# A matmul with a decayed running sum: the opening sixteen steps rearranged in banks, pieces and order

## The chip, the cores and the metric

The kernel runs on one core of a Trainium2 chip. Its time is the device time of one execution in microseconds (us), the median over several executions; lower is better. The profile is one execution recorded by the hardware profiler, and all instants below count from the start of its span.

## The reference

```
x: (16, 2048, 1024)  w: (1024, 1024)  decay: (1024,)      float32
xw = x @ w
out[:, 0] = xw[:, 0]
for t in range(1, 2048):
    out[:, t] = decay * out[:, t - 1] + xw[:, t]
```

So there is one large matrix product and, along each batch's time axis, a first-order recurrence in every one of the 1024 output columns.

## The kernel before

**Tiling.** The 16 x 2048 rows of x are cut into 64 chunks of 512 rows, and two neighbouring chunks make a group. The 1024 output columns are cut into eight heads of 128 (n = 0 to 7; head n belongs to half h = n // 4 of the columns). The contraction is cut into eight blocks k = 0 to 7, where k = 2m + e: m is one of four column blocks of x, and e says which of two interleaved columns it is. One step is one head of one group: sixteen matmuls of 128 x 512 (eight k, two chunks) into a PSUM tile of two banks. There are 248 such steps, and the last group is worked chunk by chunk in 16 half-size steps. Products have the output columns on the partitions and time along the free axis, so the recurrence is a scan along the free axis.

**PSUM.** Three two-bank tiles turn in a ring named `ps`; `spare` is one bank, and `dec2`, the squared decay, takes the eighth bank. In the first group, heads 0 to 2 use the three `ps` tiles, and head 3 has `spare` for its first chunk and the next tile of the `ps` ring for its second.

**Engines.** POOL issues the loads of x with a cast to bf16 (L105, four DMAs for a chunk, one for each quadrant of the partitions) and most of the loads of w (L245). VectorE (DVE) turns a chunk by 32 x 32 blocks (L115, 32-bit elements, so pairs of bf16 stay together), and a copy parts the pairs into the layout that TensorE reads (L123): on ScalarE (ACT) in the steady state, and split between ACT and DVE in the first two chunks. w lands in staging tiles and is "settled" into its place by sixteen copies (L253), numbered 8h + 4e + m; copy number i must be there before the heads of half h can use block k = 2m + e.

**After the matmuls** a tile goes one of two ways. Unpaired: DVE scans all of it straight out of PSUM (L194). Paired: ACT copies it to `xs` (L168) and scales its even columns by the decay into `h` (L158), POOL adds (L174), DVE scans the odd columns alone with the squared decay (L180), ACT scales that result (L158), and POOL adds the even columns (L208). A PSUM tile is free after the scan L194, or after the pair L168 and L158. Heads 3 and 7 are unpaired, heads 0 and 1 of the first group too. Then DVE turns the result back (L215), and SP stores four heads at a time with four DMAs (L228).

**Order.** Every instruction is pinned to program order, and each engine runs its own instructions strictly in that order. The order of all work but the matmuls is written by hand for the first 17 steps, in the dictionary `agenda` (L320); step 8 has an empty entry. Entry -99 comes ahead of all steps; entry s comes behind the matmuls of step s. Later steps follow a fixed rule (`usual`). The letters: M loads half a chunk of x, U a part of w, L the next quadrant of a later chunk. W and w settle a piece of w on DVE and on ACT. E turns half a chunk; F (DVE) and G (ACT) part it. T turns a whole chunk, X and Y part its two halves on ACT. P is the ACT and POOL work ahead of a scan, S the scan, C what completes a tile, B the turn back, D makes the decay columns and their squares.

**The opening.** 34 matmuls on zeros (L262) keep TensorE busy until the first data. Then, for chunk 0, heads 0 to 3: the even k of its first half, the even k of its second half, and the odd k over its full width. Then heads 0 to 2 of chunk 1 by halves, and head 3 of chunk 1 (step 3). Step 4 is the first that uses the second half of w.

Of the kernel before, what the change touches and what calls it, by code (L numbers as in the profile page):

```python
# [25 lines left out]
def kernel(  # L26
# [63 lines left out]
    dec2 = psp.tile([128, 512], FP32, name="dec2")  # L90
# [19 lines left out]
    def turn(c, j0=0, j1=NJ):  # L110
        if c not in xw_of:
            xw_of[c] = ring(sb, "xw", 2, [128, M, NJ, P, 2], BF16)
        src = xb_of[c][:, j0:j1].rearrange("p j c -> p (j c)").bitcast(FP32)
        dst = xw_of[c].rearrange("p m j i e -> p (m j i e)").bitcast(FP32)
        pin(nc.vector.transpose(  # L115
            out=dst.rearrange("p (m j i) -> p j m i", m=M, i=P)[:, j0:j1],
            in_=src.rearrange("p (j m c) -> p j m c", m=M, c=P)))
# [18 lines left out]
    class Tile:  # L136
# [3 lines left out]
        def __init__(self, g, n, ps, ot, there):  # L140
            self.b, self.t0 = chunks[g[0]]
            self.T = TL * len(g)
            self.n, self.ps, self.ot, self.there = n, ps, ot, there
            self.final = g == [nch - 1]
            self.paired = n % R != R - 1
            if len(tiles) in flips or len(tiles) - len(slots) in flips:
                self.paired = not self.paired
            self.so = ring(sb, "so", 4, [128, 2 * TL + 2])
            self.prev = None if self.t0 == 0 else last[n]
            if self.t0 + self.T < S:  # L150
                last[n] = const.tile([128, 1], FP32, name=f"keep{n}", bufs=2)
                self.keep = last[n]
            else:
                self.keep = None
# [22 lines left out]
        def scan(self):  # L177
            T, n, so = self.T, self.n, self.so
            if self.paired:
                pin(nc.vector.tensor_tensor_scan(  # L180
                    out=so[:, 3:T + 2:2],
                    data0=dec2[:, n:n + 1].to_broadcast([128, T // 2]),
                    data1=self.xs[:, 1:T:2],
                    initial=0.0 if self.prev is None else self.prev,
                    op0=ALU.mult,
                    op1=ALU.add,
                ))
            else:
                parts = self.ps if isinstance(self.ps, tuple) else (self.ps,)
                size = T // len(parts)  # L190
                before = 0.0 if self.prev is None else self.prev
                for i, ps in enumerate(parts):
                    t = 2 + i * size
                    pin(nc.vector.tensor_tensor_scan(  # L194
                        out=so[:, t:t + size],
                        data0=dec[:, n:n + 1].to_broadcast([128, size]),
                        data1=ps,
                        initial=before,
                        op0=ALU.mult,
                        op1=ALU.add,  # L200
                    ))
                    before = so[:, t + size - 1:t + size]
# [10 lines left out]
        def back(self):  # L213
            T, n = self.T, self.n
            pin(nc.vector.transpose(  # L215
                out=self.ot[:, :, n % R * P:(n % R + 1) * P],
                in_=self.so[:, 2:T + 2].rearrange("p (i t) -> p i t", t=P)))
            self.there.add(n)
            size = 2 if self.final and n >= R else R
            n0 = n // size * size  # L220
            if self.there.issuperset(range(n0, n0 + size)):
                self.store(n0, n0 + size)

        def store(self, n0, n1):
            c0 = n0 % R * P
            size = (n1 - n0) * P
            for q in (0, 2, 1, 3):
                pin(nc.sync.dma_start(  # L228
                    out=_ap(out, [[D, P], [P * D, self.T // P], [1, size]],
                            (self.b * S + self.t0) * D + n0 // R * CH + q * CR + c0),  # L230
                    in_=self.ot[quad(q), :, c0:c0 + size]))
# [29 lines left out]
    for _ in range(34):  # L261
# [16 lines left out]

    def settle_one(i, copy):
        settle(i // 8, i // 4 % 2, i % 4, copy)  # L280

    def decays(i):
# [3 lines left out]
        pin(nc.vector.tensor_tensor(out=dec2[:, 0:K], in0=dec, in1=dec, op=ALU.mult))  # L286
# [6 lines left out]
    def turn_and_load(c):  # L293
# [19 lines left out]
        "E": lambda i: turn(i // 2, *halves[i % 2]),  # L313
        "F": lambda i: part(i // 2, nc.vector.tensor_copy, 0, 2, *halves[i % 2]),
        "G": lambda i: part(i // 2, nc.scalar.copy, 2, M, *halves[i % 2]),
        "f": lambda i: part(i // 2, nc.vector.tensor_copy, 2, M, *halves[i % 2]),
        "D": decays,
        "L": lambda i: load(*loads.pop(0)) if loads else None,
    }
    agenda = {  # L320
        -99: "M0 M1 U0 U1 M2 M3 U2 U3 L L L W0 w1 E0 F0 G0 w3 W2 E1 F1 G1 W4 w5 W6 w7 E2 F2 D G2 E3 F3 G3 W8 W9 W10 W11",
        0: "w12 L L w13 P0 S0",
        1: "w14 L P1 L",
        2: "S1 W15 P2 B0 S2",
        3: "T2 L S3 C0 C1 C2",
        4: "L P4 X2 L Y2 L B2 T3 B1 L",
        5: "P5 C3 X3 L S4",
        6: "B3 L Y3 S5 L P6 C5 C4 T4",
        7: "S7 S6 X4 L C7 C6 B5 B4 B7",
        8: "",  # L330
        9: "P8 B6 S8 P9 L L T5 C8",
        10: "P10 L L S9 L C9 L B8",
        11: "X5 S10 L C10 S11 B9",
        12: "P12 L B11 B10 C11 Y4",
        13: "P13 S12 T6 Y5 C12 L",
        14: "S13 P14 C13 L B12 L L",
        15: "S15 X6 S14 C14 B13",
        16: "L P16 B14 B15 Y6 L L",
# [43 lines left out]
    perform(agenda[-99].split())  # L382
    for step, (g, n) in enumerate(slots):
        T = TL * len(g)
        if n % R == 0:
            ot, there = ot_tile(NJ * len(g)), set()
        if step == 0:
            heads = [ring(psp, "ps", 3, [128, T]) for _ in range(3)]
            firsts = [ps[:, 0:TL] for ps in heads] + [spare]
            for j0, j1 in halves:  # L390
                for k in range(0, K, 2):
                    for i in range(R):
                        matmul(firsts[i], i, k, xt_of[0], j0 * P, j1 * P)
            for k in range(1, K, 2):
                for i in range(R):
                    matmul(firsts[i], i, k, xt_of[0])
            for j0, j1 in halves:
                for i in range(3):
                    for k in range(K):
                        matmul(heads[i][:, TL:T], i, k, xt_of[1], j0 * P, j1 * P, j0 * P)  # L400
        if step < R:
            if n < 3:
                ps, second = heads[n], heads[n][:, TL:T]
            else:
                second = ring(psp, "ps", 3, [128, TL])
                ps = (spare, second)
            if n >= 3:
                for k in range(K):
                    matmul(second, n, k, xt_of[1])
        else:  # L410
# [4 lines left out]
            for k in range(K):  # L415
                for l, c in enumerate(g):
                    matmul(ps[:, l * TL:(l + 1) * TL], n, k, xt_of[c])
        tiles.append(Tile(g, n, ps, ot, there))
        left = step - len(slots)
# [31 lines left out]
```

## Time and profile before

| | us |
|---|---|
| median of 7 runs | 915.01 (914.55 to 915.71) |
| the profiled execution | 915.01 |
| its span, first to last instruction | 913.2 |
| PE busy | 894.8 (98%) |
| DVE busy | 826.2 (90%) |
| ACT busy | 686.0 (75%) |
| POOL busy | 664.4 (73%) |
| a 128 x 1024 turn back (L215, 248 of them) | 1.217 each |
| a 128 x 2048 turn of a chunk (L115, 62) | 2.286 each |
| a copy parting half a chunk on ACT (L123, 124) | 1.903 each |
| a paired tile on ACT: L168, L158 | 1.012, 0.694 each |

Busy times overlap between engines. A group row of the profile gives the line, the engine, the operation, output<-input with shapes and the count; after the bar come the busy time, the mean of one in ns, and the idle time of the engine just ahead of such instructions, with what ended most of it. A timeline row gives the start, the duration from the first to the last of the instructions merged in it, and in brackets the idle time ahead of it with its releaser. Matmul ends are modelled, so distances from start to start are the safer measure of TensorE's rate.

### The profile page before, as it was taken

Reading aid. Unit: us, or ns where it says so; the run is one execution under the profiler, and the core shown is the slowest. Engines: PE = TensorE matmul, PEld = TensorE weight load, DVE = VectorE, ACT = ScalarE, POOL = GpSimd, SP = SyncE. Lnnn points to the kernel's source line nnn. Section 1 sums busy time; section 2 is a strip of 40 time slices with the busy share of each in tenths; the row PEclk is TensorE's granted clock in tenths of the full one; section 3 lists DMA queues with packets and bytes.
Section 4 is the critical chain, followed back from the end, with each engine's and each line's share of the span. In section 5 each row is a group of like instructions: output and inputs, shape, how many; then the busy total and the mean of one; then the engine's idle time right before and its main releaser. Section 6 shows DMA issues by size and latency. Waiting matters only on the chain.

```text
span 913.2 us, 12008 instructions
## 1 busy us (share of the span) xinstructions
PE 894.8 (98%) x4170; PEld 408.3 (45%) x4170; DVE 826.2 (90%) x613; ACT 686.0 (75%) x950; POOL 664.4 (73%) x764
## 2 busy tenths in 40 slices
PE   8899999999999999999999999999999999999995
PEld 4444444444444444444444444444444444444442
DVE  4999999999999999999998999999999999999986
ACT  3778877877777778778778778778778778777753
POOL 8688878677777777777677777777787786775552
PEclk9999999999999999999999999999999999999998
DMA  9999999999999999999999999999999999999668
GB/s 171 166 220 215 215 242 259 241 253 247 237 252 250 232 233 233 221 230 234 223 233 228 226 228 231 227 227 231 226 227 230 230 231 223 231 231 208 149 152 217
DMA packets 406253, 204.49 MB, mean 224 GB/s; under 512 B 12976, under 2 KB 405936, under 8 KB 406192
## 3 DMA queue, kind: packets, MB, share of 16 engines
q1 hardware_dynamic: 268848, 134.76, 59.7%
q0 software_dynamic: 137344, 68.96, 56.6%
q8 instruction: 32, 0.52, 0.2%
q14 instruction: 29, 0.24, 0.1%
HBM read 138.42 MB, written 134.22 MB: 299 GB/s over the span
## 4 chain that ended last, share of the span: by engine, by line
PE 91%; DMA 3%; POOL 2%; DVE 2%; issue 1%; ACT 1%; SPq 0%; DVEq 0%; POOLq 0%
PE ps L126 90%; DMA xb<-in_x_dram 2%; POOL xb L105 1%; POOL ot L245 1%; DVE so L194 1%; DVE xw L115 1%; PE spare L126 0%; DMA out_dram<-ot 0%; DVE so L180 0%; POOL so L208 0%; ACT xt L123 0%; DVE ot L215 0%; POOL xs L174 0%; ACT xs L168 0%; SPq L228 0%
## 5 line engine op out<-in xcount | busy, mean ns | idle before, releaser
L126 PE MATMUL ps<-xt,wsb 128*128 128x512 bf16 (+1 forms) x4092 | 878.6, 377 | 6.1 <-DVE so L194 3.4
L126 PEld LDWEIGHTS <-wsb 128*128 128x128 bf16 x4136 | 404.6, 98 | 487.0 <-issue 6.5
L174 POOL TENSOR_TENSOR xs<-h,xs 128x512 f32<-128x512 f32 (+1 forms) x193 | 245.4, 1271 | 196.2 <-ACT h L158 87.7
L168 ACT COPY xs<-ps 128x1024 f32<-128x1024 f32 (+1 forms) x193 | 191.6, 993 | 160.3 <-PE ps L126 158.0
L215 DVE STREAM_TRANSPOSE ot<-so 128x1024 f32<-128x1024 f32 (+1 forms) x264 | 302.8, 1184 | 2.0 <-POOL so L208 1.1
L208 POOL TENSOR_TENSOR so<-h,xs 128x512 f32<-128x512 f32 (+1 forms) x193 | 244.1, 1265 | 33.6 <-ACT h L158 17.3
L123 ACT COPY xt<-xw 128x2048 bf16<-128x2048 bf16 (+1 forms) x128 | 239.9, 1876 | 7.6 <-DVE xw L115 7.6
L105 POOL DMA_DIRECT2D xb<-in_x_dram x264 | 174.1, 660 | 2.8 <-DMA ot<-in_w_dram 1.2
L158 ACT ACTIVATE h<-so,dec 128x512 f32<-128x512 f32 (+1 forms) x193 | 147.3, 763 | 34.5 <-DVE so L180 30.6
L115 DVE STREAM_TRANSPOSE xw<-xb 128x2048 f32<-128x2048 f32 (+1 forms) x66 | 146.7, 2223 | 5.5 <-DMA xb<-in_x_dram 5.4
L180 DVE TENSOR_TENSOR_SCAN so<-dec,keep,xs 128x512 f32<-128x512 f32 (+1 forms) x99 | 121.7, 1230 | 30.3 <-POOL xs L174 30.1
L180 DVE TENSOR_TENSOR_SCAN so<-dec,xs 128x512 f32<-128x512 f32 x94 | 114.9, 1222 | 31.7 <-POOL xs L174 28.6
L158 ACT ACTIVATE h<-ps,dec 128x512 f32<-128x512 f32 (+1 forms) x193 | 132.0, 684 | 0.0
L194 DVE TENSOR_TENSOR_SCAN so<-dec,ps 128x1024 f32<-128x1024 f32 x33 | 74.5, 2261 | 0.0
L194 DVE TENSOR_TENSOR_SCAN so<-dec,keep,ps 128x1024 f32<-128x1024 f32 (+1 forms) x33 | 73.4, 2224 | 0.0
L211 ACT COPY keep<-so 128x1 f32<-128x1 f32 x136 | 25.1, 187 | 0.3 <-DVE so L194 0.3
L173 ACT COPY so<-keep 128x1 f32<-128x1 f32 x99 | 19.0, 192 | 0.7 <-DVE ot L215 0.7
L171 POOL MEMSET so<- 128x1 f32 x94 | 11.0, 117 | 3.2 <-DVE ot L215 3.2
L126 PE MATMUL spare<-xt,wsb 128*128 128x512 bf16 (+1 forms) x44 | 11.3, 360 | 0.0
L245 POOL DMA_DIRECT2D ot<-in_w_dram x16 | 8.9, 554 | 2.3 <-issue 0.7
L262 PE MATMUL spare<-idle 128*128 128x512 bf16 x34 | 9.3, 444 | 1.2 <-DVE idle L259 1.2
L253 ACT COPY wsb<-ot 128x512 bf16<-128x512 bf16 x6 | 3.4, 616 | 6.3 <-DMA ot<-in_w_dram 6.3
(18 smaller groups left out, 19.9 us busy)
## 6 DMA issues: line engine op xcount, KB each, us to landing
out_dram<-ot SPq DMA_DIRECT2D x248, 512.0 KB, 10.8
xb<-in_x_dram POOLq DMA_DIRECT2D x248, 256.0 KB, 7.8
out_dram<-ot SPq DMA_DIRECT2D x12, 256.0 KB, 4.3
xb<-in_x_dram POOLq DMA_DIRECT2D x16, 128.0 KB, 5.1
ot<-in_w_dram POOLq DMA_DIRECT2D x12, 128.0 KB, 5.1
out_dram<-ot SPq DMA_DIRECT2D x8, 128.0 KB, 2.9
ot<-in_w_dram SPq DMA_DIRECT2D x4, 128.0 KB, 3.6
ot<-in_w_dram POOLq DMA_DIRECT2D x4, 64.0 KB, 4.4
```

The source lines that it names most:

```text
L105: pin(nc.gpsimd.dma_start(out=xb_of[c][quad(q), j0:j1], in_=_ap(x, [[D, P], [P * D, j1 - j0], [1, CQ]], (b * S + t0 + j0 * P) * D + q * CQ)))
L115: pin(nc.vector.transpose(out=dst.rearrange("p (m j i) -> p j m i", m=M, i=P)[:, j0:j1], in_=src.rearrange("p (j m c) -> p j m c", m=M, c=P)))
L123: pin(copy(out=xt_of[c][:, m0:m1, :, j0 * P:j1 * P], in_=src))
L126: pin(nc.tensor.matmul(out=ps[:, t0:t1], lhsT=wsb[:, k, n].rearrange("p q i -> p (q i)"), rhs=xt[:, k // 2, k % 2, t0:t1], start=(k == 0 a ...
L158: pin(nc.scalar.activation(out=h, in_=src, func=mybir.ActivationFunctionType.Copy, scale=dec[:, self.n:self.n + 1]))
L168: pin(nc.scalar.copy(out=self.xs, in_=self.ps))
L174: pin(nc.gpsimd.tensor_tensor(out=self.xs[:, 1:T:2], in0=g, in1=self.xs[:, 1:T:2], op=ALU.add))
L180: pin(nc.vector.tensor_tensor_scan(out=so[:, 3:T + 2:2], data0=dec2[:, n:n + 1].to_broadcast([128, T // 2]), data1=self.xs[:, 1:T:2], init ...
L194: pin(nc.vector.tensor_tensor_scan(out=so[:, t:t + size], data0=dec[:, n:n + 1].to_broadcast([128, size]), data1=ps, initial=before, op0=A ...
L208: pin(nc.gpsimd.tensor_tensor(out=so[:, 2:T + 2:2], in0=h, in1=self.xs[:, 0:T:2], op=ALU.add))
L211: pin(nc.scalar.copy(out=self.keep, in_=so[:, T + 1:T + 2]))
L215: pin(nc.vector.transpose(out=self.ot[:, :, n % R * P:(n % R + 1) * P], in_=self.so[:, 2:T + 2].rearrange("p (i t) -> p i t", t=P)))
```

## The change

It leaves the arithmetic of the result and the steady state as they are and rewrites the opening, up to step 16:

- `dec2` leaves PSUM at first: the squares stand in SBUF (`squares`), and deed `d` writes them again, in step 8, into a bank that is free by then. That bank, `spare1`, holds the second chunk of head 3 until its scan. So all four heads have a bank for each of the first two chunks, and head 3 takes no tile of the `ps` ring any more.
- A half chunk is turned in two pieces (m 0-1, m 2-3) and parted in four, m 0 and 2 on DVE, m 1 and 3 on ACT.
- The matmuls on zeros go from 34 to 27, and the first waits for a small ACT copy that is placed ahead of everything, so that ACT's table load comes at the start.
- Chunk 0: k = 0 and 2 of both halves come first, then k = 4, 6, 1, 3, 5, 7 over the full width. Chunk 1 is worked for four heads. In steps 4 to 7 the even k come ahead of the odd ones, and in step 8 all of the third chunk ahead of the fourth.
- The agenda of the opening is another one. The pieces of w for heads 4 to 7 and odd k are all settled by ACT, in the order 15, 13, then (behind tile 2's copies) 12, 14.
- Stores go through a new class `Outlet`; the last two pairs of heads get an output tile each.

```diff
@@ decay squares
-    dec2 = psp.tile([128, 512], FP32, name="dec2")
+    squares = [const.tile([128, K], FP32, name="squares")]
@@ turn
-    def turn(c, j0=0, j1=NJ):
+    def turn(c, j0=0, j1=NJ, m0=0, m1=M):
...
-            out=dst.rearrange("p (m j i) -> p j m i", m=M, i=P)[:, j0:j1],
-            in_=src.rearrange("p (j m c) -> p j m c", m=M, c=P)))
+            out=dst.rearrange("p (m j i) -> p j m i", m=M, i=P)[:, j0:j1, m0:m1],
+            in_=src.rearrange("p (j m c) -> p j m c", m=M, c=P)[:, :, m0:m1]))
@@ scan, paired
-                    data0=dec2[:, n:n + 1].to_broadcast([128, T // 2]),
+                    data0=squares[-1][:, n:n + 1].to_broadcast([128, T // 2]),
@@ outlets
+        def __init__(self, ns, nj, half=0, queues=(nc.sync,)):
+            self.ns, self.missing, self.half = ns, set(ns), half
+            self.nj, self.t0, self.queues = nj, half * nj * P, queues
+            self.ot = ot_tile(nj)
@@ opening
+    pin(nc.scalar.copy(out=idle[:, 0:1], in_=idle[:, 1:2]))
-    for _ in range(34):
+    for _ in range(27):
...
+    def part_one(i, copy):
+        part(i // 8, copy, i % 4, i % 4 + 1, *halves[i // 4 % 2])
...
+    def square_again(i):
+        squares.append(ring(psp, "spare1", 1, [128, TL]))
+        square(0)
...
-        "E": lambda i: turn(i // 2, *halves[i % 2]),
-        "F": lambda i: part(i // 2, nc.vector.tensor_copy, 0, 2, *halves[i % 2]),
-        "G": lambda i: part(i // 2, nc.scalar.copy, 2, M, *halves[i % 2]),
+        "E": lambda i: turn(i // 4, *halves[i // 2 % 2], i % 2 * 2, i % 2 * 2 + 2),
+        "F": lambda i: part_one(i, nc.vector.tensor_copy),
+        "G": lambda i: part_one(i, nc.scalar.copy),
@@ agenda
-        -99: "M0 M1 U0 U1 M2 M3 U2 U3 L L L W0 w1 E0 F0 G0 w3 W2 E1 F1 G1 W4 w5 W6 w7 E2 F2 D G2 E3 F3 G3 W8 W9 W10 W11",
-        0: "w12 L L w13 P0 S0",
-        1: "w14 L P1 L",
-        2: "S1 W15 P2 B0 S2",
-        3: "T2 L S3 C0 C1 C2",
-        4: "L P4 X2 L Y2 L B2 T3 B1 L",
-        5: "P5 C3 X3 L S4",
-        6: "B3 L Y3 S5 L P6 C5 C4 T4",
-        7: "S7 S6 X4 L C7 C6 B5 B4 B7",
...
-        9: "P8 B6 S8 P9 L L T5 C8",
-        10: "P10 L L S9 L C9 L B8",
-        11: "X5 S10 L C10 S11 B9",
-        12: "P12 L B11 B10 C11 Y4",
-        13: "P13 S12 T6 Y5 C12 L",
-        14: "S13 P14 C13 L B12 L L",
-        15: "S15 X6 S14 C14 B13",
-        16: "L P16 B14 B15 Y6 L L",
+        -99: "M0 M1 U0 U1 M2 M3 U2 U3 W0 w1 L E0 F0 G1 E1 L F2 D G3 E2 F4 L G5 W2 E3 F6 w3 G7 W4 W6 w5 w7 E4 F8 G9 E5 F10 G11 E6 F12 G13 E7 F14 G15 W8 W10 W9 W11",
+        0: "P0 L w15 w13",
+        1: "L L L S0 C0",
+        2: "L P2 P1 w12 S1 L L B0 B1 S2",
+        3: "w14 C2 T2",
+        4: "S3 P4 X2 Y2 T3 C1",
...
+        6: "L L P5 L B3 L L S4 L S5 B2 C3 X3 Y3 C4 T4",
+        7: "P6 C5 S7 X4 S6",
+        8: "C7 C6 L d P8 B4 B7 B6",
+        9: "B5 P9",
+        10: "L S8 P10 C8 T5 X5 L S9",
+        11: "L L S11 L C9 Y4 S10 C10 B8",
...
+        13: "B11 P12 B10 B9 Y5 S12 P13 C12",
+        14: "L P14 T6 S13 C13 L Y6 L",
+        15: "L S15 L S14 C14",
+        16: "B13 B12 B15 B14 P16 X6",
@@ matmuls
+    spares = [spare] + [ring(psp, "spare1", 1, [128, TL])]
...
+            outlets = [Outlet(ns, nj)]
+        if left in (-R, 2 - R):
+            outlets = [Outlet(range(n, n + 2), nj)]
...
-            firsts = [ps[:, 0:TL] for ps in heads] + [spare]
+            firsts = [ps[:, 0:TL] for ps in heads] + [spares[0]]
+            seconds = [ps[:, TL:T] for ps in heads] + [spares[1]]
             for j0, j1 in halves:
-                for k in range(0, K, 2):
+                for k in (0, 2):
                     for i in range(R):
                         matmul(firsts[i], i, k, xt_of[0], j0 * P, j1 * P)
-            for k in range(1, K, 2):
+            for k in (4, 6, 1, 3, 5, 7):
                 for i in range(R):
                     matmul(firsts[i], i, k, xt_of[0])
-            for j0, j1 in halves:
-                for i in range(3):
-                    for k in range(K):
-                        matmul(heads[i][:, TL:T], i, k, xt_of[1], j0 * P, j1 * P, j0 * P)
+            for k0 in range(0, K, 4):
+                for i in range(R):
+                    for k in range(k0, k0 + 4):
+                        matmul(seconds[i], i, k, xt_of[1], 0, H * P)
+            for i in range(R):
+                for k in range(K):
+                    matmul(seconds[i], i, k, xt_of[1], H * P, TL, H * P)
...
+            todo = [(k, l) for k in range(K) for l in range(len(g))]
+            if step < K:
+                todo.sort(key=lambda kl: kl[0] % 2)
+            elif step == K:
+                todo.sort(key=lambda kl: kl[1])
```

## The prediction

> **What bounds the kernel now.** I read the page's busy times, then the waits of TensorE (PE), then its timeline. The page gives PE 894.8 of 913.2 us; the waits view says what ended its idle times, in total, count and longest:
>
> ```profile
> PE ps L126 <- DVE so L194: 3.4, 4, 1.3
> PE ps L126 <- DVE xt L123: 1.4, 2, 0.8
> PE ps L126 <- DVE wsb L253: 1.3, 1, 1.3
> ```
>
> Together 6.1 us. The PE timeline shows where the larger ones lie (start, duration, work, wait ahead of it):
>
> ```profile
> 27.35 1.89 PE L126 MATMUL ps<-xt,wsb 128*128 128x512 bf16 x8 [1.25 <-DVE so L194]
> 29.52 7.07 PE L126 MATMUL ps<-xt,wsb 128*128 128x512 bf16 x32 [0.29 <-DVE so L194]
> 37.87 27.79 PE L126 MATMUL ps<-xt,wsb 128*128 128x512 bf16 x128 [1.28 <-DVE so L194]
> 66.24 9.01 PE L126 MATMUL ps<-xt,wsb 128*128 128x512 bf16 x41 [0.58 <-DVE so L194]
> ```
>
> See that 66.24 follows the last stall: from step 14 to its last matmul PE never waits. The chain of waits agrees:
>
> ```profile
> 66.24 813.42 PE ps L126 x3768
> ```
>
> That is 0.2159 us a matmul, 3.454 a step. The tail behind PE follows it: SP's waits from 840 us on are 25.7 us for DVE's turns back, so stores aren't what holds the end. What PE is ahead by when step 14 starts should therefore be the gain, one for one. All depends on the first 66 us: real matmuls start at 10.38, and the seven stalls to 66.24 sum to 6.1.
>
> These rows set the opening, since the changed program's order leaves POOL's first 35 instructions, all early loads among them, as they are:
>
> ```profile
> 23.88 1.22 DVE L253 COPY wsb<-ot 128x512 bf16<-128x512 bf16 x4 [0.62 <-DMA ot<-in_w_dram]
> 25.02 4.45 DVE L194 TENSOR_TENSOR_SCAN so<-dec,ps 128x1024 f32<-128x1024 f32 x2
> 27.34 1.66 ACT L253 COPY wsb<-ot 128x512 bf16<-128x512 bf16 x3 [3.72 <-DMA ot<-in_w_dram]
> 28.90 1.00 ACT L168 COPY xs<-ps 128x1024 f32<-128x1024 f32 x1
> 29.81 0.69 ACT L158 ACTIVATE h<-ps,dec 128x512 f32<-128x512 f32 x1
> ```
>
> The brackets give landings: w for heads 4-7, even k, at 23.8; odd k at 27.3. The same view has DVE or ACT starting on landings at 8.30 (x, first half of chunk 0), 12.35 (w, k = 4, 6), 15.80 (w, odd k), 18.52 and 21.29 (chunk 1).
>
> **Part by part, up to step 4.**
>
> *Warm-up.* The table load (1.28 us) from about 0.87, a copy of 0.2: the first matmul on zeros moves from 1.20 to about 2.45. The 34 took 9.18 us to 10.38; at 0.216 they'd take 7.34, so 1.84 went to a slow start of 8 or 9 at 0.427. 27 then end at 2.45 + 5.83 + 1.84 = 10.1. The Trainium skill (TensorE: Matmul & The Clock Gate, What's actually happening) speaks against this: the clock opens after a busy window of 3.4 us which runs free, so after up to 6.8 us; that makes 16 slow ones, end 11.7. The row gives 10.1, the rule at worst 11.7; I take the row. It matters little: PE waits for data at 12.2 and w at 16.2 anyway.
>
> *Finer pieces.* Half-size turns: 128 x 512 took 0.68 (L215); the half copies I set at 0.42 on DVE and 0.62 on ACT (between half of 0.69 and 1.04 and the whole; w's 128 x 512 ACT copy took 0.62). Then: first piece ready 8.30 + 0.68 + 0.42 = 9.4; the second half's at 12.1 (six DVE instructions stand between them); k = 4 waits for DVE to 13.7; k = 1 for w at 15.8, so 16.16 against 16.33 before. 16 matmuls: 19.6. Chunk 1's first piece is there at 18.52 + 1.12 = 19.65; from there PE runs unbroken (64 half-width matmuls, 0.108 each) to **26.6**, with all eight head-chunks done. Before, that point was 29.1: chunk 1 began at 20.55, and head 3 stood from 25.7 to 27.35 for a bank.
>
> *Step 4's bank.* `ps` comes free after DVE's scan of head 0, which stands behind four w copies: 25.02 to 27.27 as now. Step 4 starts at **27.35** instead of 29.52. The 0.7 us wait also means that errors in the paragraphs above cost nothing below 0.7.
>
> *Step 4's odd k: the new wait.* Even k take 8 x 0.216, to 29.08. k = 1 needs piece 12, on ACT behind pieces 15 and 13 (0.55 each from 27.34), the keep copy (0.08), and tile 2's pair (0.91 + 0.58): it starts at 30.02 and ends at 30.64. PE waits 1.6 us, goes on at **30.7**, and starts step 5 at **32.42** (before 32.97). Queued behind piece 12: 14, ready before PE asks.
>
> **Steps 5 to 16.** Step 5's and 6's banks are free (29.5, 30.1). The 1.28 us at 37.87 falls away, since head 3 holds no `ps` tile: steps 6, 7, 8 start at 35.9, 39.3, 42.8. I walked the other queues with the rows' starts:
> - DVE: turns back of heads 0 and 1, scan 2 (31.7), turn of chunk 2 (32.8; its load has landed by 32.6), head 3's two scans, turn of chunk 3 at 38.06 (it landed just before 38 in this trace), then scans 4 and 5, chunk 4 at 44.8, scan 7 (47.0 to 49.25).
> - ACT: X2 Y2 35.1 to 38.8, tile 5 to 40.4, X3 Y3 40.4 to 44.1, tile 4's end, tile 6 44.7 to **46.3**.
>
> Step 9 needs tile 6's bank: 46.37 instead of 46.2. Step 10 needs scan 7 (49.3), PE comes at 49.8. Step 11 needs tile 8 (ACT, **52.8**), PE comes at 53.3. Steps 12 to 16 have 1.5 us and more to spare; step 14's stall of 0.58 goes, because chunk 5's loads are issued in one run (about 42 to 44.4, now 43.63 to 50.20) and the scan of tile 11 follows sooner. Chunk 4's third and fourth loads move from 37.9/38.5 to about 36.6/37.3.
>
> Step 9 was at 48.23, so PE leads by 1.86 there; 0.74 more at step 14 (66.24 against 63.64): **2.6 us**.
>
> *Squares in SBUF*, scans 2, 4, 5, 6. The row: a scan with the squares in PSUM takes 1.22 us, often beside POOL's 1.27 us adds. The Trainium skill (SBUF — State Buffer, Who interferes with whom) speaks against the change: with two SBUF inputs DVE uses the read port that GpSimd reads by, and one waits until the other is done. By the row: 0. By the rule: scan 4 (41.4) meets POOL's add for tile 5 (40.5 to 41.8) and loses 0.4, covered by step 10's slack of 0.5; without that cover 4 x 1.27 at most. I take 0.
>
> *Stores.* The last pair's output tile now is one that chunk 62 used; its store has landed by 902.6, the turn back starts at 904.8: nothing. An SBUF tile in place of the other costs nothing either.
>
> **Sum.** Span 913.2 - 2.6 = 910.6. The profiled execution took 915.01 (1.8 around its span), which is the median too: **912.4**.
>
> **Rivals.**
> 1. *More of it:* ACT and DVE run tighter than I walked them. Step 11 can't start ahead of tile 8's release, 52.75 against 55.13 + 0.74: 3.1 us; with a little there too 3.3, so 911.7. For it: my DVE and ACT chain is a sum of upper ends. Against: chunk 3's landing at 38 holds tile 6, whatever PE does.
> 2. *Taken back:* the gates at steps 9 to 11 slip by 1 to 2 us (port lock, a load landing as late as now: chunk 4's turn started at 45.73). For it: slack of only 0.1, 0.5, 0.5. A turn at 45.7 costs about 0.5; with locks on top 1.4 of the 2.6: 913.8. Here too belongs "no effect": PE's opening gain meets banks that come free no earlier.
> 3. *Slower:* chunk 4's turn stands on DVE ahead of scans 7 and 6, and its ACT half ahead of tile 8. If its loads land late, DVE stands still, scan 7 ends 4.5 us after that turn's start, and step 10 with it. Free up to 45.2; from 47.9 the whole gain is gone (52.42 is step 10's start before, less the later stall). At 49.0, 1.2 us slower: 916.2. For it: the loads took up to 7.1 us from issue now. Against: they are issued earlier, and stores start later (first full set about 44.9, before 42.3).
>
> **Chances.** Forecast 69% (1.9 to 3.1 us gained: 911.9 to 913.1), rival 1 14%, rival 2 11%, rival 3 6%. About 0.2%, 1.8 us, is what a measurement can tell: faster by more 83%, within it 11%, slower 6%. The range reaches to 911.1 for rival 1 and to 914.0 for most of rival 2; rival 3 stays out.
>
> **What would show it.** PE's timeline: no break from about 19.7 to 26.6; a start at 27.35 behind a scan L194; a wait of some 1.6 us near 29.1 ended by ACT's w copy; none near 36 to 38; little at 46; step 14 at about 63.6. Wrong if a wait near 49 to 53 is over 1 us, if loads of w land elsewhere than at 23.8 and 27.3, or if the distance from last matmul to the end of the span is not 11.1 us.

## The result, and the profile after

| us | before | after |
|---|---|---|
| median (runs of both on one chip) | 915.06 (914.22 to 916.31, 34 runs) | 913.04 (911.94 to 914.11, 14 runs) |
| ratio, 95% interval | | 0.9977 (0.9970 to 0.9984) |
| the profiled execution, its span | 915.01, 913.2 | 912.43, 910.6 |
| start of step 4, 5, 6 | 29.52, 32.97, 37.87 | 27.68, 32.62, 36.07 |
| start of step 9, 14 | 48.23, 66.24 | 46.72, 63.98 |
| start of step 40 | 156.02 | 154.21 |
| start of the last matmul, and from there to the end | 901.73, 11.5 | 899.91, 10.7 |

The kernel is faster by 2.0 us, 0.23%. The waits of TensorE in the profile after (engine, tile and line; what released it; us in total, times, longest) no longer hold the 3.4 us for `so`:

```profile
PE ps L126 <- DVE xt L123: 1.7, 3, 0.6
PE ps L126 <- ACT wsb L265: 1.3, 1, 1.3
PE ps L126 <- DVE so L194: 0.5, 2, 0.3
```

(Lines are those of the kernel that ran: L265, L167, L157, L179 and L219 of the changed kernel are L253, L168, L158, L180 and L215 of the kernel before.) Where these lie is in the timeline of TensorE:

```profile
20.17 1.47 PE L126 MATMUL ps<-xt,wsb 128*128 128x256 bf16 x12 [0.63 <-DVE xt L123]
...
27.68 1.89 PE L126 MATMUL ps<-xt,wsb 128*128 128x512 bf16 x8 [0.23 <-DVE so L194]
30.88 60.89 PE L126 MATMUL ps<-xt,wsb 128*128 128x512 bf16 x280 [1.31 <-ACT wsb L265]
92.05 18.29 PE L126 MATMUL ps<-xt,wsb 128*128 128x512 bf16 x84 [0.28 <-DVE so L194]
```

From 20.17 there is no break up to step 4. Step 4 stands 1.5 us (start to start) for w's piece 12. The stalls at 37.87 and 66.24 are gone. Two others are new: 0.29 us from start to start at 46.72, the head of step 9, too little for a row of its own, and 0.45 at 92.05, the head of step 22. ScalarE shows why k = 1 waits:

```profile
27.59 1.14 ACT L265 COPY wsb<-ot 128x512 bf16<-128x512 bf16 x2 [3.34 <-DMA ot<-in_w_dram]
28.73 1.00 ACT L167 COPY xs<-ps 128x1024 f32<-128x1024 f32 x1
29.63 0.69 ACT L157 ACTIVATE h<-ps,dec 128x512 f32<-128x512 f32 x1
30.21 1.13 ACT L265 COPY wsb<-ot 128x512 bf16<-128x512 bf16 x2
```

Pieces 15 and 13, tile 2's pair (the copy L167 and the scaling L157), and only then 12 and 14. Step 9 starts when tile 6's pair is done, and the chain of waits shows what that pair stood behind (start, us, what):

```profile
40.82 3.60 ACT xt L123 x2
44.42 0.67 ACT h L157
45.16 0.91 ACT xs L167
46.08 0.60 ACT h L157
46.72 31.25 PE ps L126 x144
```

Chunk 3's two halves, the end of tile 4, tile 6's pair: ScalarE has no gap there. VectorE's timeline has the other three places that matter:

```profile
41.68 2.64 DVE L179 TENSOR_TENSOR_SCAN so<-squares,xs 128x512 f32<-128x512 f32 x2
...
56.61 2.27 DVE L115 STREAM_TRANSPOSE xw<-xb 128x2048 f32<-128x2048 f32 x1
...
59.98 2.31 DVE L194 TENSOR_TENSOR_SCAN so<-dec,keep,ps 128x1024 f32<-128x1024 f32 x1
...
70.81 2.31 DVE L115 STREAM_TRANSPOSE xw<-xb 128x2048 f32<-128x2048 f32 x1 [1.53 <-DMA xb<-in_x_dram]
```

The two scans with squares in SBUF take 2.64 us together, 1.52 and 1.18; the turn of chunk 5 waits for nothing, and the scan of tile 11 follows it at 59.98; the turn of chunk 6 waits 1.53 us for its last load, which landed at 70.69. The scan that holds step 22, tile 19's, ends at 92.0, and what stands ahead of it on VectorE, ScalarE and GpSimd is late with that turn (the table at "Chunk 6's loads early" shows it).

The account closes: 2.26 us of lead at step 14, 0.45 given back at step 22, 0.77 from a shorter end (11.51 against 10.74), together 2.58, which is the difference of the two profiled executions. How much of the 0.77 belongs to the change is open: with the old end it took 11.0 to 11.5 us in four traces, with the new one 10.7 to 11.3 in ten.

### The profile page after: what moved, and what is told of

Same layout as the page of the kernel before. It is cut to its first block, busy times and chain, and to the rows that moved or that the text cites. A ratio compares the mean times of both kernels' runs of the same rounds, so it can differ in the third digit from the quotient of the medians.

```text
span 910.6 us, 12012 instructions
## 1 busy us (share of the span) xinstructions
PE 894.4 (98%) x4163; PEld 407.8 (45%) x4163; DVE 827.0 (91%) x621; ACT 687.3 (75%) x956; POOL 664.6 (73%) x764
## 4 chain that ended last, share of the span: by engine, by line
PE 91%; ACT 2%; POOL 2%; DVE 2%; DMA 1%; issue 1%; DVEq 0%; ACTq 0%; POOLq 0%
PE ps L126 91%; DVE so L194 1%; ACT xt L123 1%; POOL xb L105 1%; POOL ot L257 1%; DMA ot<-in_w_dram 1%; DVE ot L219 1%; ACT xs L167 1%; ACT h L157 1%; DMA xb<-in_x_dram 1%; POOL xs L173 0%; PE spare L126 0%; DVE so L179 0%; POOL so L208 0%; DVE wsb L265 0%
## 5 line engine op out<-in xcount | busy, mean ns | idle before, releaser
L167 ACT COPY xs<-ps 128x1024 f32<-128x1024 f32 (+1 forms) x193 | 191.6, 993 | 158.2 <-PE ps L126 155.5
L219 DVE STREAM_TRANSPOSE ot<-so 128x1024 f32<-128x1024 f32 (+1 forms) x264 | 302.5, 1184 | 0.7
L157 ACT ACTIVATE h<-so,dec 128x512 f32<-128x512 f32 (+1 forms) x193 | 147.2, 762 | 33.2 <-DVE so L179 29.7
L179 DVE TENSOR_TENSOR_SCAN so<-spare,keep,xs 128x512 f32<-128x512 f32 (+1 forms) x99 | 121.6, 1229 | 29.3 <-POOL xs L173 28.9
L179 DVE TENSOR_TENSOR_SCAN so<-spare,xs 128x512 f32<-128x512 f32 x90 | 110.0, 1223 | 31.3 <-POOL xs L173 28.3
L157 ACT ACTIVATE h<-ps,dec 128x512 f32<-128x512 f32 (+1 forms) x193 | 131.9, 684 | 0.0
L126 PE MATMUL spare<-xt,wsb 128*128 128x512 bf16 (+1 forms) x58 | 13.2, 342 | 0.0
L265 ACT COPY wsb<-ot 128x512 bf16<-128x512 bf16 x7 | 4.0, 616 | 4.6 <-DMA ot<-in_w_dram 4.6
```

The costliest lines, as they stand in the source:

```text
L126: pin(nc.tensor.matmul(out=ps[:, t0:t1], lhsT=wsb[:, k, n].rearrange("p q i -> p (q i)"), rhs=xt[:, k // 2, k % 2, t0:t1], start=(k == 0 a ...
L157: pin(nc.scalar.activation(out=h, in_=src, func=mybir.ActivationFunctionType.Copy, scale=dec[:, self.n:self.n + 1]))
L167: pin(nc.scalar.copy(out=self.xs, in_=self.ps))
L179: pin(nc.vector.tensor_tensor_scan(out=so[:, 3:T + 2:2], data0=squares[-1][:, n:n + 1].to_broadcast([128, T // 2]), data1=self.xs[:, 1:T:2 ...
L219: pin(nc.vector.transpose(out=outlet.ot[:, :, c0:c0 + P], in_=self.so[:, 2 + t0:2 + t0 + nj * P].rearrange("p (i t) -> p i t", t=P)))
```

## Experiments

One table first, since their traces differ in when the first loads land: chunk 3 landed between 37.54 and 39.60 us, and everything behind it shifts with it. So the last two columns are distances: from that landing to the start of step 9, and from there to the start of step 14 (five steps without a wait are 17.26).

| | ratio to before (95%) | landing to step 9 | step 9 to 14 |
|---|---|---|---|
| before | 1 | 10.29 | 18.01 |
| after | 0.9977 (0.9970 to 0.9984) | 8.53 | 17.26 |
| bank alone | 1.0028 (1.0018 to 1.0039) | 8.50 | 21.35 |
| loads alone | 1.0023 (1.0016 to 1.0030) | 10.29 | 17.43 |
| bank and loads | 1.0027 (1.0019 to 1.0036) | about 8.3 | about 19.1 |
| after, w's piece 12 first | 0.9973 (0.9962 to 0.9983) | 9.01 | 17.26 |
| after, coarse pieces | 0.9971 (0.9960 to 0.9982) | 8.98 | 17.26 |
| after, chunk 6 early | 0.9975 (0.9967 to 0.9984) | 8.74 | 17.3 |
| after, late load | 0.9981 (0.9974 to 0.9988) | 8.46 | 17.26 |
| after, late load and old scan order | 0.9976 (0.9967 to 0.9984) | 8.57 | 17.26 |
| after, chunks mixed in step 8 | 0.9975 (0.9969 to 0.9982) | 8.79 | 17.26 |
| after, squares in SBUF throughout | 1.0050 (1.0037 to 1.0064) | 8.63 | 17.3 |
| attempt 1 at a better one | 0.9979 (0.9970 to 0.9988) | 7.71 | 18.6 |
| attempt 2 | 0.9987 (0.9980 to 0.9993) | 7.72 | 18.92 |

(In the traces of four of them some 2% of the matmul records are missing; their entries are worked out from the waits.)

**The bank alone.** The kernel before, with the squares in SBUF until step 8 and the bank `spare1` for head 3's second chunk.

```diff
-    dec2 = psp.tile([128, 512], FP32, name="dec2")
+    squares = [const.tile([128, K], FP32, name="squares")]
...
-        8: "",
+        8: "d",
...
-                second = ring(psp, "ps", 3, [128, TL])
+                second = spare1
```

> The kernel before, with one part of the change: head 3 of the first group gets a bank of its own for its second chunk, and the squares stand in SBUF until step 8. Order, pieces and agenda stay. Theory G (gates): PE no longer waits near 26 and 37, reaches step 9 about 1.6 us sooner, but step 14 still needs the scan of tile 11, which stands on DVE behind the turn of chunk 5, whose last load lands at 58.05 as before; the wait ahead of step 14 grows from 0.6 to 2 us or so and step 14 starts at 66.2 as before: gain 0 to 0.3 us against before. Rival S (sum of stalls): every stall that goes is gained, 1.3 to 1.8 us.

918.22 us, 2.6 slower than before by the ratio: theory G had the place right and the size wrong. The stalls near 26 and 37 us are gone (one of 1.4 us for chunk 3's parts is new in step 8), and step 9 comes 1.8 us sooner behind chunk 3's landing. Then TensorE stands, in its timeline:

```profile
69.45 40.91 PE L126 MATMUL ps<-xt,wsb 128*128 128x512 bf16 x181 [3.50 <-DVE so L194]
```

and VectorE's timeline says why:

```profile
61.38 2.31 DVE L115 STREAM_TRANSPOSE xw<-xb 128x2048 f32<-128x2048 f32 x1 [2.23 <-DMA xb<-in_x_dram]
...
67.08 2.32 DVE L194 TENSOR_TENSOR_SCAN so<-dec,keep,ps 128x1024 f32<-128x1024 f32 x1
```

The turn of chunk 5 stands for its last load, with the scans of tiles 9, 10 and 11 behind it. That load was issued at 51.86 and landed at 61.26 (before: 50.20 and 58.05; chunk 3 landed 1.7 us later in this trace, so 1.7 of the 3.2 us are not the edit's). This execution took 919.53, 1.3 above the median, so the stall may be longer than usual. The window of TensorE behind it (us, busy time and matmuls, granted clock, DMA share, GB/s) shows that the stall costs more than its length:

```profile
70.00:74.00 4.00, 4.00 (x13) 0.58 1.30 215
```

Here eight matmuls started 0.427 us apart instead of 0.216, some 1.7 us more; from 74 us on the clock stands at 1.00 again.

**The loads alone.** The kernel before, with four loads, those of chunk 5, in one run in step 5.

```diff
-        5: "P5 C3 X3 L S4",
-        6: "B3 L Y3 S5 L P6 C5 C4 T4",
-        7: "S7 S6 X4 L C7 C6 B5 B4 B7",
+        5: "L L L L P5 C3 X3 S4",
+        6: "B3 Y3 S5 P6 C5 C4 T4",
+        7: "S7 S6 X4 C7 C6 B5 B4 B7",
```

> The kernel before, with chunk 5's four loads moved on POOL's queue in one run ahead of the add of tile 5, so that they are issued at about 39 to 42 us, before the first stores at 44.5. All else stays. Theory G: chunk 5 has landed by about 50, its turn starts at about 57.0 with no wait for a load, the scan of tile 11 ends before PE asks at 65.5, and the stall of 0.7 us at step 14 goes: 0.6 to 0.75 us faster than before. Rival S says the same; a rival in which the loads are held by bandwidth and not by their issue says 0, with chunk 5 landing near 58 again.

917.79 us: also slower, by 2.1, which no theory had. Chunk 5 was there at 54.52, and the stall ahead of step 14 fell to 0.17. But chunk 6, issued from 57.70 on as before, landed at 67.56 to 74.96, its last load 4 us later than before; VectorE and then TensorE stood, once more for 0.80 us at 96.83:

```profile
75.08 2.31 DVE L115 STREAM_TRANSPOSE xw<-xb 128x2048 f32<-128x2048 f32 x1 [4.60 <-DMA xb<-in_x_dram]
```
```profile
81.98 14.06 PE L126 MATMUL ps<-xt,wsb 128*128 128x512 bf16 x64 [2.02 <-DVE so L194]
```

The DMA view from 54 to 62 us (queue, packets, MB, share of the engines' time) tells who had the engines: q1 carries the stores, q0 the loads.

```profile
q1 hardware_dynamic: 3681, 1.86, 93.8%
q0 software_dynamic: 2, 0.00, 0.1%
```

Two packets of x in 8 us, although two loads had been out since 57.70 and 58.35. In the same stretch of the profile after, q0 moved 897 packets. My reading: a stretch without loads in the queue goes to the stores that wait, and the next loads pay.

**Bank and loads together.** Both edits in one kernel.

> The kernel before with both parts of the two runs that were slower than it when made alone: head 3's own bank, and chunk 5's loads issued in one run. Theory G: the two gates are in series, so that neither helps alone; together step 14 starts at about 65 instead of 66.2. But DVE's queue stands as it did, with the turns of chunks 5 and 6 ahead of the scans that free banks, and chunk 6's loads come as late as with the loads alone (68 to 75): the stall of 2 to 3 us at steps 18 to 22 stays, and the result is 0 to 2.5 us slower than before. Rival S: 1.3 + 0.7 us faster than before, about 913.2.

917.73 us, 2.5 slower than before, at the end of theory G's range, and no better than either alone. The profiled execution took 914.16, the lowest of its twelve times, so it shows the kind of stall and not the usual size:

```profile
42.77 6.92 PE L126 MATMUL ps<-xt,wsb 128*128 128x512 bf16 x30 [0.82 <-ACT xt L123]
...
65.09 27.79 PE L126 MATMUL ps<-xt,wsb 128*128 128x512 bf16 x126 [1.16 <-DVE so L194]
93.51 16.78 PE L126 MATMUL ps<-xt,wsb 128*128 128x512 bf16 x75 [0.64 <-DVE so L194]
```

What bank and loads bring is lost again to ScalarE's parts at step 8 and to scans at steps 14 and 22. So something else in the change is needed for the bank to pay. What is left is the order of the deeds on VectorE and ScalarE, the order of the matmuls in the opening, w's last pieces on ScalarE, and the pieces; not all of these were taken apart. The runs below start from the changed kernel and take single parts out.

**w's piece 12 ahead of tile 2.**

```diff
-        0: "P0 L w15 w13",
+        0: "P0 L w15 w13 w12",
...
-        2: "L P2 P1 w12 S1 L L B0 B1 S2",
+        2: "L P2 P1 S1 L L B0 B1 S2",
```

> The changed kernel, with the w piece 12 settled on ACT ahead of tile 2's pair instead of behind it. PE then does not wait 1.3 us for it near 29.4. Theory G: tile 2's pair and all that hangs on it (scan 2, turn of chunk 2, its parting, tile 5, chunk 3's parting, tile 6) moves 0.55 us later, so step 9's bank comes at about 47.2 instead of 46.7 and PE's lead is lost there again: 0.3 to 0.6 us slower than the changed kernel, about 913.5. Rival S: the 1.3 us are gained, about 911.7.

913.07 us, the same as the changed kernel; of theory G the later step 9 came, but not the 0.3 to 0.6 us. TensorE's timeline:

```profile
31.54 14.85 PE L126 MATMUL ps<-xt,wsb 128*128 128x512 bf16 x68 [1.00 <-ACT wsb L265]
47.16 45.05 PE L126 MATMUL ps<-xt,wsb 128*128 128x512 bf16 x208 [0.77 <-ACT h L157]
```

The wait moves from k = 1 to k = 5 (piece 14), and what is won there stands again at step 9 for tile 6's pair, which comes 0.5 us later behind the landing. The longest wait of the profile after costs nothing.

**Coarse pieces.** Half chunks turned whole and parted in two, as before the change, in the changed kernel; entry -99 is fitted to that.

```diff
-        "E": lambda i: turn(i // 4, *halves[i // 2 % 2], i % 2 * 2, i % 2 * 2 + 2),
-        "F": lambda i: part_one(i, nc.vector.tensor_copy),
-        "G": lambda i: part_one(i, nc.scalar.copy),
+        "E": lambda i: turn(i // 2, *halves[i % 2]),
+        "F": lambda i: part(i // 2, nc.vector.tensor_copy, 0, 2, *halves[i % 2]),
+        "G": lambda i: part(i // 2, nc.scalar.copy, 2, M, *halves[i % 2]),
```

> The changed kernel with the first two chunks turned by whole halves and parted by two m at a time, as before; bank, order of matmuls, w and agenda behind stay. Theory G: chunk 1's first product starts at about 20.95 instead of 20.17, the eight head-chunks end near 27.9, step 4 starts at about 28.0 instead of 27.7, and all of it vanishes in the wait for the w piece 12, so that step 4 goes on at 30.9 as in the changed kernel: the same within 0.2 us. Rival S: the pieces are worth what PE waits more, 0.8 us slower than the changed kernel.

912.99 us, the same. Chunk 1 starts 0.75 us later (20.92 against 20.17) and step 4 0.5 later, but:

```profile
30.98 15.71 PE L126 MATMUL ps<-xt,wsb 128*128 128x512 bf16 x72 [0.88 <-ACT wsb L265]
```

k = 1 goes on at 30.98 against 30.88. The wait for piece 12 is cover for all that stands ahead of it.

**Chunk 6's loads early.** All four in step 7, at 50.67 to 52.61; entries 10 and 11 issue three fewer.

```diff
-        7: "P6 C5 S7 X4 S6",
-        8: "C7 C6 L d P8 B4 B7 B6",
+        7: "P6 C5 L L L L S7 X4 S6",
+        8: "C7 C6 d P8 B4 B7 B6",
```

> The changed kernel with chunk 6's four loads issued in one run, right behind tile 5's completion on POOL (about 49 to 52 us instead of 53 to 61). In the changed kernel its turn waits 1.5 us for the last of them at 70.8, DVE is late from there, and PE loses 0.45 us at step 22. Theory G: with the loads there early the turn does not wait and the 0.45 us at step 22 go: 0.3 to 0.5 us faster than the changed kernel. Rival T (transfers): loads and first stores share the DMA engines, an earlier chunk 6 only makes stores or chunk 7 later, and a wait of the same size comes back in steps 15 to 30: no gain, or a loss up to 1 us.

912.85 us. The last load landed at 65.78 instead of 70.69, and no wait is left behind step 9, that of step 22 included. That the wait at step 22 was chunk 6's load is shown by six traces with these loads in their old place: the later they land, counted from the start of step 14, the longer TensorE stands there, nearly one for one.

| | from step 14 to the landing | stall at step 22 |
|---|---|---|
| late load | 6.15 | none |
| coarse pieces | 6.42 | 0.14 |
| piece 12 first | 6.60 | 0.33 |
| late load and old scan order | 6.67 | 0.41 |
| after | 6.71 | 0.45 |
| chunks mixed in step 8 | 6.97 | 0.73 |

Still, rival T is half right: most of what VectorE gains stands again one chunk on. Chunk 7's last load lands no sooner (84.85 us; 83.37 in the profile after, where all landings are some 1.2 us earlier), and its turn waits for it:

```profile
84.97 2.31 DVE L115 STREAM_TRANSPOSE xw<-xb 128x2048 f32<-128x2048 f32 x1 [1.82 <-DMA xb<-in_x_dram]
```

Tile 19's scan ends some 0.25 us ahead of TensorE. The 0.45 us that the edit should bring can't be told apart in the medians (0.2 us, intervals overlapping).

**One load of chunk 5 late,** and then the **old order of scans** as well.

```diff
-        6: "L L P5 L B3 L L S4 L S5 B2 C3 X3 Y3 C4 T4",
-        7: "P6 C5 S7 X4 S6",
+        6: "L L P5 L B3 L L S4 S5 B2 C3 X3 Y3 C4 T4",
+        7: "P6 C5 L S7 X4 S6",
@@ the second kernel only
-        11: "L L S11 L C9 Y4 S10 C10 B8",
+        11: "L L S10 S11 L C9 Y4 C10 B8",
```

> The changed kernel with chunk 5's fourth load issued at about 49.3 us instead of 44.0, as late as in the kernel before (50.2). Theory L (the prediction's: the loads in one run make the scan of tile 11 early enough, and so take the last stall, that ahead of step 14, away): the load lands at about 58, as before; the turn of chunk 5 starts 1.4 us later, the scan of tile 11 ends 1.4 us later, and a stall of 0.5 to 0.8 us comes back ahead of step 14: 0.5 to 0.8 us slower than the changed kernel. Rival O (the new order, in which the scan of tile 11 stands ahead of that of tile 10, is enough by itself): the scan of tile 11 ends at 63.5 us, TensorE comes at 64.0, no stall: within 0.2 us of the changed kernel.

> The late load of the run before, and also the scan of tile 10 ahead of that of tile 11 again, as in the kernel before. By rival O both covers are then gone: the scan of tile 11 ends at about 64.7 us and TensorE waits 0.6 to 0.8 us ahead of step 14, so 0.6 to 0.8 us slower than the changed kernel. By theory L this is as slow as the late load alone, no more. A third reading, that the opening behind step 9 has more slack than I think, gives no stall here either.

913.20 and 913.09 us: both as the changed kernel. VectorE's timeline of the first, and of the second:

```profile
56.79 2.31 DVE L115 STREAM_TRANSPOSE xw<-xb 128x2048 f32<-128x2048 f32 x1 [0.27 <-DMA xb<-in_x_dram]
...
60.18 2.32 DVE L194 TENSOR_TENSOR_SCAN so<-dec,keep,ps 128x1024 f32<-128x1024 f32 x1
```
```profile
59.39 2.41 DVE L179 TENSOR_TENSOR_SCAN so<-spare,keep,xs 128x512 f32<-128x512 f32 x2
61.72 2.31 DVE L194 TENSOR_TENSOR_SCAN so<-dec,keep,ps 128x1024 f32<-128x1024 f32 x1
```

The load, issued 5.1 us later, landed only 2.7 later (56.66), so the turn waited 0.27. Tile 11's scan ends at 62.5 in the first and 64.03 in the second, and TensorE comes to step 14 at 63.89 and 64.56. Neither the late fourth load nor this scan order brings the stall back; the third reading, more slack than expected, holds. It is not all of the old state: the other three loads stay early, and the turn back of tile 8, which stood ahead of both scans before, stays behind them.

**The chunks mixed in step 8.**

```diff
-            elif step == K:
-                todo.sort(key=lambda kl: kl[1])
```

> The changed kernel, but step 8 takes the third and fourth chunk in turn for every k, as the kernel before does. Theory N (the part is worth nothing): the first half of the fourth chunk, k = 0 to 3, is parted by 42.5 us and TensorE asks at 43.2; the second half is parted by 44.45 and asked for at 44.9: no stall over 0.3 us at step 8, and step 9 waits for its bank until 46.7 anyway; same time within 0.3 us. Rival T (the part carries a piece of the gain): the second half is late by 0.5 to 1 us in most executions and step 9's bank does not hide it: 0.4 to 1 us slower.

913.02 us, the same: no wait in step 8, and step 9 stands 0.55 us for tile 6's pair as expected of theory N. (At step 22 this trace has 0.73, by the table above for chunk 6's load.)

**The squares in SBUF throughout.** Deed `d` is left out, so the squares stay where every paired scan reads them beside `xs`.

```diff
-        8: "C7 C6 L d P8 B4 B7 B6",
+        8: "C7 C6 L P8 B4 B7 B6",
```

> The changed kernel without the deed that writes the squares of the decay into PSUM in step 8, so that all paired scans read both inputs from SBUF. In the changed kernel one of the four scans that do so met a POOL add and took 1.52 instead of 1.18 us. Theory L (lock): each of some 185 scans that meets an add waits for its end, or holds the add back; with adds on POOL over half of the time and DVE 90% busy that is 0.3 to 0.7 us a scan, and DVE comes to be the bound of every group: 10 to 60 us slower than the changed kernel. Rival: the longer scan was an accident, and the time is the same within 1 us.

919.78 us (four runs), 6.7 slower than the changed kernel, below theory L's 10 to 60. By operation (busy us, mean ns; idle time ahead), first this kernel, then the changed one:

```profile
L179 DVE TENSOR_TENSOR_SCAN so<-squares,keep,xs 128x512 f32<-128x512 f32 x90 | 150.1, 1667 | 0.5
```
```profile
L179 DVE TENSOR_TENSOR_SCAN so<-spare,keep,xs 128x512 f32<-128x512 f32 x90 | 115.2, 1280 | 28.1 <-POOL xs L173 27.8
```

A scan takes 0.39 us more, and VectorE's idle time goes with it. TensorE stands once at length:

```profile
96.28 13.95 PE L126 MATMUL ps<-xt,wsb 128*128 128x512 bf16 x56 [3.58 <-DVE so L194]
```

Again the seven to eight matmuls behind such a stall are 0.427 us apart. Later one wait of 0.83 us is all that shows: the steady state takes the longer scans, the first 96 us do not.

**Two attempts at a better kernel.** Both put pieces 12 and 14 on VectorE between its first scans, and what completes tile 4 behind tile 6's pair. The first also issues chunk 5's and 6's loads early and puts chunk 4's turn behind the scan of tile 6, its part on ScalarE between the pairs of tiles 8 and 9; the second leaves chunk 4's turn ahead of tile 7's scan and issues only chunk 6's loads early. What they share, and then entries 6 to 8 of each:

```diff
-        1: "L L L S0 C0",
+        1: "L L L S0 W12 W14 C0",
...
-        4: "S3 P4 X2 Y2 T3 C1",
+        4: "S3 P4 X2 Y2 T3 C1 B1",
...
-        6: "L L P5 L B3 L L S4 L S5 B2 C3 X3 Y3 C4 T4",
-        7: "P6 C5 S7 X4 S6",
-        8: "C7 C6 L d P8 B4 B7 B6",
@@ the first
+        6: "L L L L L L P5 S4 B3 S5 B2 C3 X3 Y3",
+        7: "P6 C4 C5 L L L L S7 S6 T4",
+        8: "C7 C6 d P8 X4 B4 B7 B6",
@@ the second
+        6: "L L P5 L B3 L L S4 L S5 B2 C3 X3 Y3",
+        7: "P6 C4 T4 C5 L L L L S7 X4 S6",
+        8: "C7 C6 d P8 B4 B7 B6",
```

> The changed kernel with another order in steps 1 to 10: the w pieces 12 and 14 are settled by DVE between the scans of heads 0 and 1, so that neither PE nor tile 2's pair waits for them; the turn back of head 1 stands behind the turn of chunk 3; tile 6's pair stands ahead of tile 4's end on ACT; scans 7 and 6 stand ahead of the turn of chunk 4; chunk 5's loads are issued ahead of tile 5's add and chunk 6's in one run. Theory G: step 5 starts at 31.1 instead of 32.6, step 9 at about 46.1 instead of 46.7 (chunk 3's parting ends at 44.4), step 11 at 53.0 instead of 53.6; with no wait for chunk 6, 0.6 to 1.1 us faster than the changed kernel, about 912.1. Rival T: chunk 6 or a store is late instead and takes it back: the same or slower.

> The changed kernel with w's pieces 12 and 14 copied by VectorE between its first two scans, what completes tile 4 behind tile 6's pair on ScalarE, and chunk 6's loads in one run ahead of step 8. If the walk is right: no wait near 29 us, step 9's bank at 45.9 instead of 46.7, no wait at step 12, none at step 22: 0.8 to 1.2 us faster than the changed kernel, 912.0. Rival V (VectorE has no slack from 38 us to the scan of tile 11, so what is gained ahead of it is lost again at step 14): step 14 starts within 0.3 us of the changed kernel's 64.0, and only the 0.45 us of step 22 is gained, 912.6.

913.24 and 913.92 us: the first no better than the changed kernel, the second slower. Step 9 comes 0.8 us sooner behind the landing in both, as the walk had it. It is lost again: in the first TensorE stands 1.18 us at step 12 (58.47) for tile 9's pair, which stands on ScalarE behind the part of chunk 4, in the second 1.46 us at step 10 (51.93) for tile 7's scan. In the second, VectorE starts that scan at 49.63 instead of 47.58, 1.1 us later once its 0.95 us later landing is taken off: the turn back of head 1, moved out of the first 31 us, is worth 1.2 there. That is rival V's reason, though four steps sooner and with a larger loss than it said. Attempt 2 also stands 0.39 at step 22, where none was expected: chunk 6 had landed at 66.42, but chunk 7's turn waited 2.03 us for its load. What 0.8 us at step 9 is worth with both avoided wasn't tried.

## Why the prediction was right, step by step

It said 912.4 us (911.1 to 914.0), from 2.6 of lead; measured are 913.04, and 2.0 between the medians, near the low end of the forecast's 1.9 to 3.1. Of its signs of being wrong, none showed at 49 to 53 us; w's loads landed up to 0.5 us off, and the end behind the last matmul was 0.8 shorter than before, so these two came in small.

*Warm-up.* The sum took the row's 8 or 9 slow matmuls (10.1 us) over the rule of the Trainium skill (TensorE: Matmul & The Clock Gate, What's actually happening), from whose free-running window it estimated 11.7 at worst. The rule has the better of it: in the profile after the first 14 matmuls on zeros are slow, in the kernel with mixed chunks 8 are; all 27 took 8.89 and 7.48 us, from 2.28 on in both. It cost nothing, as was said: products of x start at 11.01 or 9.65, and step 4 at 27.68 or 27.29.

*Finer pieces.* Predicted 0.68, 0.42 and 0.62, measured 0.71, 0.43 and 0.62. Chunk 1 started at 20.17, not 19.65, since its first half was there at 18.94, not at 18.52. "Errors cost nothing below 0.7" held, and the coarse kernel shows that the pieces are worth nothing that could be measured here.

*Step 4 and the new wait.* 27.68 against 27.35; k = 1 at 30.88 against 30.7; step 5 at 32.62 against 32.42. Right, 0.2 to 0.3 late, with w's loads, which landed 0.25 to 0.5 later. The wait was rightly charged at nothing beyond that: piece 12 first brought nothing.

*Step 9.* 46.72 against 46.37, tile 6's pair on ScalarE as predicted. The gate was right.

*Step 14.* 63.98 against 63.64; the 0.74 us stall went whole. The time was right, **the reason given was the smaller part**: "because chunk 5's loads are issued in one run". VectorE before:

```profile
58.17 2.31 DVE L115 STREAM_TRANSPOSE xw<-xb 128x2048 f32<-128x2048 f32 x1 [1.16 <-DMA xb<-in_x_dram]
...
63.87 2.32 DVE L194 TENSOR_TENSOR_SCAN so<-dec,keep,ps 128x1024 f32<-128x1024 f32 x1
```

Tile 11's scan starts 3.89 us sooner after (59.98). The turn of chunk 5 is 1.56 of it (56.61). The other 2.33 is VectorE's order: the scan of tile 10 and the turn back of tile 8 no longer stand between that turn and the scan. TensorE comes 2.26 us sooner, so my estimate from these figures is that the loads without the order would leave a stall of 0.7 us, and the order without the loads hardly one. Neither was run in full: with one load 5 us later, and with the scan of tile 10 put back as well, 1.4 and 0.5 us were left between tile 11's scan and TensorE (1.7 in the changed kernel).

*Behind step 14.* "PE never waits" was taken over from before and is the term that failed: 0.45 us at step 22, from chunk 6's last load. I had not walked past step 16. So the term "2.6" is 2.26 (the opening came 0.34 late, with landings 0.25 to 0.5 late) less 0.45, 1.81, and the median's 2.0 agrees with that. That the profiled execution still came out at the predicted 910.6 is chance: the end behind the last matmul was 10.7 us long there, and 10.7 to 11.3 in the other kernels with the same end.

*Squares in SBUF.* Taken as 0, by the row, against the Trainium skill (SBUF — State Buffer, Who interferes with whom). The row was no evidence: before, the squares were in PSUM. The rule's 0.4 at tile 4's scan came as 1.52 us against 1.18, and as 1.78 and 1.99 in the kernels with mixed chunks and with piece 12 first. It was covered, as the sum had said; with the squares left in SBUF the longer scans lack cover at 96 us.

*Rivals.* "More of it" had ScalarE and VectorE tighter; both attempts show how little room there is. "Taken back" and "slower" named the right resource, a chunk's loads that land late ahead of scans; in the changed kernel it took 0.45 us, at chunk 6 and not 4, in the bank alone it took all and more.

## What to carry to other kernels

A bank and a run of loads each made the kernel slower, alone and together, and are part of one that is faster: the earlier TensorE is, the sooner it meets the next queue. Walk a moved opening until the schedule repeats, and not only to the last stall of the old trace. And when several edits go in together, undo each in the new kernel as well as doing it in the old one: here the pieces, the order in step 8 and one load of the run undone one at a time, and that load with the scan of tile 10 together, moved nothing that could be measured, so none of them may be named as the gain. Not run were the changed kernel without the bank, and with all of the old order on VectorE and ScalarE; that these two carry the gain together is argued from the traces, not shown.

## What the runs showed of the hardware

- After a wait of 3.50 us (the bank alone) and one of 3.58 us (squares in SBUF) TensorE's granted clock was 0.58 over 4 us, and seven to eight matmuls started 0.427 us apart: 1.7 us on top. Waits of 1.46 (attempt 2) and 2.02 us (the loads alone) had no such sequel. The Trainium skill (TensorE: Matmul & The Clock Gate, What's actually happening) puts the idle window at about 3.4 us, which fits these four. But one long wait is not needed. In the bank-alone trace the clock also fell at 15.3 us, behind waits of no more than 1.29 us in a stretch where TensorE was busy for 1.28 of 3.40 us (the rows are as in the window above). A like stretch in the kernel before, busy for 1.66 of 3.40 us from 11.8 on, had no sequel: its clock was 1.00. What tips it isn't shown.

```profile
11.90:15.30 3.40, 1.28 (x11) 1.00 1.08 162
15.30:18.70 3.40, 3.40 (x17) 0.50 1.31 162
```

- At the start the clock opens after 8 (mixed chunks) to 14 (after) slow matmuls, though the first starts at 2.28 us in both.
- VectorE and GpSimd hold each other up both ways: a scan with squares in SBUF that met an add took 1.52 us instead of 1.18, and in the bank-alone trace GpSimd's add from 44.05 took 2.08 us instead of 1.29, while such a scan ran until 45.05.
- With stores of 512 KB in hand, loads issued by GpSimd moved two packets from 54 to 62 us (the loads alone), although two of them had been out since 57.70 and 58.35.
- The last of w's first loads landed anywhere from 26.84 to 28.90 us. The rest of the opening shifts with it: the changed kernel's own times span 911.94 to 914.11.
